# An encoder layer in hi/low fp32 parts: the residual of the down stage spread over more steps, a norm's bias added with the first eviction, the low parts on VectorE, loads kept one fewer ahead, and one norm moved into the middle stage

## The chip, the cores and the metric

The kernel runs on one core of one Trainium2 chip. The metric is the device time of one execution in microseconds (us). Before the change the median of 3 runs is 1983.87 us, from 1979.57 to 1990.23. The engines are named as the profile names them: PE is TensorE (matmul), PEld its weight loads, DVE VectorE, ACT ScalarE, POOL GpSimd, SP SyncE, whose queue issues the DMAs of this kernel.

## The reference

One encoder layer is computed for two independent sequences (s = 0, 1) of 512 tokens, with model width 1024 and inner width 2816, all in fp32:

```python
h = layer_norm(a * x + 0.5 * swiglu(x, ffn1_wg, ffn1_wu, ffn1_wd), ln1_g, ln1_b)
proj = h @ w_in                      # gq, gk, gv, gr, zf, zb, aq, ak, av
o_gla = gla_mixer(gq, gk, gv, gr, zf, zb, ...)      # bidirectional gated linear attention
o_att = gqa_mixer(aq, ak, av, q_norm_g, k_norm_g)   # grouped-query attention with rotary positions
mix = concat([o_gla, o_att]) @ w_out
h = layer_norm(a * h + mix, ln2_g, ln2_b)
h = layer_norm(a * h + 0.5 * swiglu(h, ffn2_wg, ffn2_wu, ffn2_wd), ln3_g, ln3_b)
return h + sigmoid(h @ w_pg + b_pg) * (p @ w_pe)
# swiglu(x, w_g, w_u, w_d) = (silu(x @ w_g) * (x @ w_u)) @ w_d;  a = 2 ** 0.25
```

## The kernel before

**Products in three parts.** Each fp32 operand is kept as a high part `hi` (rounded by a copy to fp32r) and a low part `lo = raw - hi`. A product is three matmuls: hi·hi, hi·lo, lo·hi. `split` (L135) makes the two parts: ACT copies the high part (L137), and VectorE or GpSimd subtracts (L138). Loads of weights go through `raw` buffers (L149, DMAs on SP's queue) and their parts into `w` buffers, of which there are six. `prefetch` (L158) keeps four finished `w` pieces and up to three raw loads ahead.

**The stages.** In order of time: the first SwiGLU (up products to about 462 us, down products to about 666 us), the middle (projections, attention, linear attention, output projection, to about 1215 us), the second SwiGLU (up to about 1629 us, down to about 1860 us), and the final gate (to the end).

**The down stage.** It uses a scheme of seven products for each 2x2 block, as in Strassen's method, in the order `ORDER = (0, 1, 4, 5, 6, 3, 2)`. Eleven row pairs of the down weight are dealt with as three groups of three (`GROUPS`) and a tail of two (`TAIL`). Three groups times seven products are 21 steps, n = 0 to 20, each with 4 x 9 = 36 matmuls (L536). For each step and row pair `w_ops` makes the operand that this product needs: for products 4, 5, 6 and 3 GpSimd first adds or subtracts two quarters of the raw rows in place (L269, one operation for each of the three row pairs), then ACT makes the high part and DVE or POOL the low part. `LOW_DOWN = (0, 1, 6, 2)` names the products whose low parts go to DVE; those of 4, 5 and 3 go to POOL. Two of the tail's operations join the steps of the second and third group. At the end of each quarter of a step `evac` moves one PSUM bank into Y: the first time that a piece of Y is written it is a copy on ACT (L526), afterwards an addition on DVE (L523). The banks are two sets of four, `pm` and `pd`.

**The residual.** The input r of the SwiGLU is loaded from DRAM, one 128x1024 tile for each s and t, and added as Y += 2·ALPHA·r (L617, on DVE). In the second down stage r is a normalized tile without its gain and bias, so `affine` first multiplies by a row g (L642) and adds a row b (L643). In `down` these eight pieces, `res(s, t)`, are due at step 4 (s = 0) or 6 (s = 1) and taken at j = 4 and j = 9 of a step, so two in each of the steps 4 to 7.

**The norm and the projections.** When Y is complete, `ln(s)` finds mean and variance and normalizes in place (L639). `flip` transposes Y on PE, applies gain and bias in the transposed form, and splits it into h1T (L661, L662), the operand of the projections. `h1_rows(s)` applies gain and bias to the untransposed rows (L642, L643) and stores them to DRAM as `sp_h`. The projections run in the order akvz(0), aq(0), gr(0), gr(1), akvz(1), ... Each is `tok_group` (L707), 32 positions of 6 matmuls, with its evacuation at the last four pieces; gr's is a SiLU on ACT (L749) into one of three `ev` buffers, which are stored to DRAM as `sp_G` (L744) by SP's queue.

**What sets the order.** The order on PE is written out by hand. A `Ticker` counts positions of the main work, and side work is woven in at positions given as numbers: `main.weave(h1_rows(0), 4, 28)` spreads four pieces up to position 28. On the other engines and on SP's queue the framework's scheduler sets the order when the program is built. Each engine then works its list in order, and an instruction that waits holds up all behind it.

Of the kernel before, what the change touches and what calls it, by code (L numbers as in the profile page):

```python
# [8 lines left out]
F32 = mybir.dt.float32  # L9
# [11 lines left out]
NT = 4  # L21
# [32 lines left out]
LOW_UP = (1, 5, 2)  # L54
LOW_DOWN = (0, 1, 6, 2)

# [14 lines left out]
class Layer:  # L71
# [88 lines left out]
    def prefetch(self):  # L160
        while len(self.ready) < 4 and (self.raws or self.queue):
            r = self.raws.pop(0) if self.raws else self.raw(self.queue.pop(0))
            n = r.shape[1] // 2
            self.ready += [self.piece(r[:, :n]), self.piece(r[:, n:])]
        while len(self.raws) < 3 and self.queue:
            self.raws.append(self.raw(self.queue.pop(0)))
# [157 lines left out]
    def down_work(self, i, place, spare):  # L324
# [21 lines left out]
        def op_tail(p, k):  # L346
# [3 lines left out]
            return None, f  # L350
        out = [load(p, 0) for p in GROUPS[0]] + [load(p, 1) for p in GROUPS[0]]
        for n, gr in enumerate(GROUPS):
            nxt = GROUPS[n + 1] if n + 1 < len(GROUPS) else None
            if n > 0:
                out += [load(TAIL[n - 1], e) for e in range(2)]
            for k in ORDER:
                for j, p in enumerate(gr):
                    out.append(op(p, k))
                    if k == 3 and nxt:
                        out.append(load(nxt[j], 0))  # L360
                    if k == 2 and nxt:
                        out.append(load(nxt[j], 1))
                if n > 0:
                    out.append(op_tail(TAIL[n - 1], k))
        return out

# [143 lines left out]

    def down(self, hs, hp, residual, ln):

# [5 lines left out]
        def evac(s, t, dd, bank):  # L518
# [5 lines left out]
            else:  # L524
                touched.add((s, t, dd))
                nc.scalar.activation(yv, bank, AF.Copy)  # L526

# [18 lines left out]
        for n in range(21):  # L546
# [8 lines left out]
            for j, _ in enumerate(product(k, H, D, NT, lambda m, t: (m, t))):  # L555
                if n >= 3 and j % 5 == 4 and residual:
                    residual[0][0] <= n and residual.pop(0)[1]()
                yield
# [5 lines left out]
        for s in range(2):  # L564
# [6 lines left out]
            if s == 0:  # L571
                self.prefetch()
                next(first)
        for _ in ln(1):
            pass

# [6 lines left out]
    def ffn(self, i, ysrc, ln, have=(), mid=None, rows=None):  # L583
# [18 lines left out]
        with P("hp", 13) as hp:  # L602
# [6 lines left out]
            g = rows(hp) if rows else None  # L609

            def res(s, t):
                r = hp.tile([128, 2, 512], F32R, tag="h", name="r").bitcast(F32).rearrange("p a n -> p (a n)")
                self.nc.sync.dma_start(r, ysrc(s, t))
                if g:
                    self.affine(r, *g)
                y = self.Y[s, t]
                self.nc.vector.scalar_tensor_tensor(y, r, 2.0 * ALPHA, y, ALU.mult, ALU.add)  # L617
            todo = [(4 if s == 0 else 6, lambda s=s, t=t: res(s, t)) for s in range(2) for t in range(NT)]
            yield from self.down(hs, hp, todo, ln)

# [523 lines left out]
def build(tc, d, outs):  # L1144
    nc = tc.nc
    ctx = ExitStack()
    with ctx:
# [36 lines left out]
        with ExitStack() as mctx:  # L1184
# [27 lines left out]
            main.place(first, (1, 5, 9, 13))  # L1212
            main.weave(h1_rows(0), 4, 28)
            main.weave(L.flip(1, 1, "h1T"), 8, 60)
            main.weave(h1_rows(1), 4, 76)

# [69 lines left out]
        def rows2(hp):  # L1286
            t = [hp.tile([128, 1024], F32, tag="h", name="lnr") for _ in range(2)]
            return [L.row(2, j, t[j]) for j in range(2)]
        for s in range(2):
# [8 lines left out]
        with ExitStack() as fctx:  # L1298
# [11 lines left out]
            def finish():  # L1310
                for s in range(2):
                    for dd in range(2):
# [4 lines left out]
                        for t in range(NT):  # L1317
# [5 lines left out]
                            for c in range(0, 512, n):  # L1323
# [9 lines left out]
                                nc.vector.tensor_tensor(gc, gc, L.Y[s, t][:, oc], ALU.add)  # L1333
                                nc.sync.dma_start(outs[s][t * 128:(t + 1) * 128, oc], gc)
            main = Ticker(finish())
            main.place(first, (2, 7, 12, 17))
# [92 lines left out]
```

## Time and profile before

| | |
|---|---|
| median of 3 runs | 1983.87 us |
| lowest, highest | 1979.57, 1990.23 us |
| profiled execution | 1983.58 us |
| its span in the trace | 1981.8 us |
| mean granted TensorE clock | 0.981 of full speed |
| busy in the span: PE, DVE, POOL, ACT | 1879.1, 1367.1, 950.2, 883.4 us |

The trace covers one execution, the one that took 1983.58 us. Its span is 1.8 us shorter, which is what lies around it. Busy time is a sum over stages that differ; what a stage waits for is read from that stage alone. Rows of the timeline give start, duration, engine, line, operation, tiles and count, and in square brackets the idle time before them and what released them.

### The profile page before, as it was taken

To read this page: it belongs to the slowest core of one execution; us is meant where nothing else is said; L and a number is where in the kernel's file an instruction comes from. 1 tells how busy PE (TensorE), PEld (TensorE's weight loads), DVE (VectorE), ACT (ScalarE), POOL (GpSimd) and SP (SyncE) were. 2 spreads that over 40 slices of the span, in tenths; PEclk is the share of its full clock that TensorE was granted. 3 is DMA by queue.
4 is the path that set the end of the run, shared out by engine and by line. 5 is a ranking of instruction groups with operands and counts; after the bars stand their busy time and mean duration, and the time that the engine had idled before them with its cause. 6 is when DMAs were issued, how large, how long until landed. Compare 5 with 4: busy or idle time off the path is not lost. (4 is left out here: it accounts for less than half of the span.)

```text
span 1981.8 us, 25356 instructions
## 1 busy us (share of the span) xinstructions
PE 1879.1 (95%) x8838; PEld 1534.9 (77%) x8838; DVE 1367.1 (69%) x2068; ACT 883.4 (45%) x1670; POOL 950.2 (48%) x710
## 2 busy tenths in 40 slices
PE   7999999999999797989998888999999999799999
PEld 5788888888788686877876667888888888588787
DVE  7856566574656974778778879566566575855973
ACT  5445444444221444757852337445444444221342
POOL 0665565554761254342234343654665555762253
PEclk9999999999999998999999999999999999899999
DMA  4425444478666233222443331435434478576142
GB/s 177 156 105 177 168 150 152 148 288 337 268 248 211 73 126 111 77 80 91 133 143 101 94 117 66 158 109 185 161 141 170 155 297 338 206 267 255 54 128 85
DMA packets 104959, 322.22 MB, mean 163 GB/s; under 512 B 11008, under 2 KB 38400, under 8 KB 99456
## 3 DMA queue, kind: packets, MB, share of 16 engines
q1 hardware_dynamic: 104832, 320.61, 44.9%
q8 instruction: 70, 1.15, 0.2%
q14 instruction: 57, 0.47, 0.1%
HBM read 218.85 MB, written 101.71 MB: 162 GB/s over the span
## 5 line engine op out<-in xcount | busy, mean ns | idle before, releaser
L138 POOL TENSOR_TENSOR w<-raw,w 128x512 fp32r<-128x512 f32 (+1 forms) x372 | 511.4, 1385 | 773.8 <-ACT w L137 714.7
L137 ACT ACTIVATE w<-raw 128x512 fp32r<-128x512 f32 (+1 forms) x586 | 363.5, 624 | 444.5 <-POOL raw L269 107.8
L425 PE MATMUL pm<-X,w 128*128 128x512 f32 x1848 | 435.0, 393 | 11.0 <-ACT X L137 8.2
L269 POOL TENSOR_TENSOR raw<-raw 128x512 f32<-128x512 f32 x240 | 348.0, 1458 | 155.6 <-DMA raw<-in_wgu 81.7
L425 PEld LDWEIGHTS pm<-X,w 128*128 128x128 f32 x1848 | 347.9, 189 | 89.5 <-ACT X L137 8.8
L425 PE MATMUL pd<-X,w 128*128 128x512 f32 x1320 | 309.2, 392 | 2.9 <-DVE w L138 2.2
L138 DVE TENSOR_TENSOR w<-raw,w 128x512 fp32r<-128x512 f32 x214 | 220.3, 1035 | 126.0 <-ACT w L137 116.4
L425 PEld LDWEIGHTS pd<-X,w 128*128 128x128 f32 x1320 | 248.5, 189 | 58.0 <-DVE w L138 3.0
L536 PE MATMUL pm<-w,XB 128*128 128x512 f32 x864 | 202.5, 394 | 5.5 <-POOL w L138 5.4
L707 PE MATMUL pm<-w,h1T 128*128 128x512 f32 (+1 forms) x768 | 183.9, 382 | 22.6 <-ACT gr L749 11.4
L536 PEld LDWEIGHTS pm<-w,XB 128*128 128x128 f32 x864 | 163.3, 190 | 42.8 <-POOL w L138 9.1
L138 DVE TENSOR_TENSOR hs<-sg,hs 128x512 fp32r<-128x512 f32 (+1 forms) x182 | 143.8, 810 | 49.5 <-ACT hs L137 48.4
L137 ACT ACTIVATE hs<-sg 128x512 fp32r<-128x512 f32 (+1 forms) x182 | 98.4, 561 | 164.8 <-DVE sg L391 64.4
L707 PEld LDWEIGHTS pm<-w,h1T 128*128 128x128 f32 x768 | 135.9, 194 | 45.0 <-ACT gr L749 11.7
L536 PE MATMUL pd<-w,XB 128*128 128x512 f32 x648 | 151.2, 393 | 15.5 <-issue 14.8
L536 PEld LDWEIGHTS pd<-w,XB 128*128 128x128 f32 x648 | 122.8, 190 | 42.0 <-issue 15.2
L523 DVE TENSOR_TENSOR Y<-Y,pm 128x512 f32<-128x512 f32 x104 | 70.6, 684 | 61.5 <-PE pm L536 61.3
L523 DVE TENSOR_TENSOR Y<-Y,pd 128x512 f32<-128x512 f32 x88 | 59.9, 684 | 60.0 <-PE pd L536 57.3
L707 PE MATMUL pm<-w,h3T 128*128 128x512 f32 x384 | 90.8, 393 | 0.9 <-DVE h3T L662 0.9
L371 DVE TENSOR_TENSOR sg<-u,pm 128x512 f32<-128x512 f32 x22 | 15.1, 687 | 109.3 <-PE pm L425 109.3
L707 PEld LDWEIGHTS pm<-w,h3T 128*128 128x128 f32 x384 | 71.2, 188 | 15.8 <-DVE h3T L662 1.4
L652 ACT ACTIVATE pd<-pd,c_lnT 128x512 f32<-128x512 f32 x48 | 36.0, 752 | 100.4 <-PE pd L650 100.4
(237 smaller groups left out, 2554.0 us busy)
## 6 DMA issues: line engine op xcount, KB each, us to landing
hs<-hs SPq DMA_DIRECT2D x126, 512.0 KB, 2.6
XB<-hs SPq DMA_DIRECT2D x42, 1536.0 KB, 6.8
raw<-in_wgu SPq DMA_DIRECT2D x88, 512.0 KB, 3.5
raw<-in_wd SPq DMA_DIRECT2D x36, 512.0 KB, 6.4
hs_t<-hs SPq DMA_DIRECT2D x56, 256.0 KB, 2.5
XB<-hs_t SPq DMA_DIRECT2D x26, 512.0 KB, 5.2
raw<-in_wout SPq DMA_DIRECT2D x16, 512.0 KB, 3.6
raw<-in_wpg SPq DMA_DIRECT2D x16, 512.0 KB, 3.5
```

Source lines behind the costliest of these rows:

```text
L137: first = nc.scalar.activation(hi, raw, AF.Copy)
L138: (eng or nc.vector).tensor_tensor(lo, raw, hi.bitcast(F32), ALU.subtract)
L269: (sums or self.nc.gpsimd).tensor_tensor(o(), x(), y(), ALU.subtract)
L371: add = lambda o, x, y: nc.vector.tensor_tensor(o, x, y, ALU.add)
L425: nc.tensor.matmul(bank, w[:, a, kt * 128:(kt + 1) * 128], X[k][:, kt, b], start=(k in (0, 1, 4) and kt == 0 and m == 0), stop=(kt == 3 an ...
L523: nc.vector.tensor_tensor(yv, yv, bank, ALU.add)
L536: nc.tensor.matmul(b[t], h[:, a, t * 128:(t + 1) * 128], d[:, c], start=(k in (0, 4, 1) and g == 0 and x == 0), stop=(g == len(H) - 1 and ...
L652: nc.scalar.activation(p, p, AF.Identity, scale=self.lnT[:, c:c + 1], bias=self.lnT[:, c + 8:c + 9])
L707: nc.tensor.matmul(banks[t][:, :width], x[:, i, t * 128:(t + 1) * 128], w[a][:, j], start=(q == 0 and a == 0 and m == 0), stop=(q == nq - ...
```

## The change

1. All low parts of the down stage go to DVE (`LOW_DOWN = ORDER`).
2. `prefetch` keeps two raw loads ahead instead of three.
3. The tail's loads and operations stand in one list, and two of them are put behind each of the positions from the eleventh on, instead of one operation with every product.
4. The residual uses two fixed tiles `rt`. A load (`fetch`) and an addition (`res`) are separate entries with half steps as due times, taken at j = 5 and j = 11: the first two loads at half step 3, the later ones at 2n+6, the addition at 2n+9, for n = 0 to 7.
5. In the second down stage the bias row is multiplied by 2·ALPHA once and added by DVE with the first eviction, in place of ACT's copy; r is then only multiplied by g.
6. The norm of s = 1 is kept as `self.later`. After the first down stage it runs at position 32 of the projections, behind akvz(0); `h1_rows(0)`, `flip(1)` and `h1_rows(1)` are spread up to positions 48, 84 and 100, before 28, 60 and 76. After the second down stage it runs behind the loads of the final gate.

```diff
-LOW_DOWN = (0, 1, 6, 2)
+LOW_DOWN = ORDER
@@ prefetch
-        while len(self.raws) < 3 and self.queue:
+        while len(self.raws) < 2 and self.queue:
@@ down_work
+        side = [x for p in TAIL for x in [load(p, 0), load(p, 1)] + [op_tail(p, k) for k in ORDER]]
         for n, gr in enumerate(GROUPS):
             nxt = GROUPS[n + 1] if n + 1 < len(GROUPS) else None
-            if n > 0:
-                out += [load(TAIL[n - 1], e) for e in range(2)]
-            for k in ORDER:
+            for m, k in enumerate(ORDER):
...
-                if n > 0:
-                    out.append(op_tail(TAIL[n - 1], k))
-        return out
+                if 7 * n + m >= 10:
+                    out += side[:2]
+                    del side[:2]
+        return out + side
@@ down, evac
                 touched.add((s, t, dd))
-                nc.scalar.activation(yv, bank, AF.Copy)
+                if rows:
+                    nc.vector.tensor_tensor(yv, bank, rows[1][:, dd * 512:(dd + 1) * 512], ALU.add)
+                else:
+                    nc.scalar.activation(yv, bank, AF.Copy)
@@ down
-                if n >= 3 and j % 5 == 4 and residual:
-                    residual[0][0] <= n and residual.pop(0)[1]()
+                if j in (5, 11) and residual and residual[0][0] <= 2 * n + j // 6:
+                    residual.pop(0)[1]()
...
-        for _ in ln(1):
-            pass
+        self.later = ln(1)
@@ ffn
+            rt = [hp.tile([128, 1024], F32, tag="h", name="r") for _ in range(2)]
+            def fetch(s, t):
+                self.nc.sync.dma_start(rt[t % 2], ysrc(s, t))
             def res(s, t):
-                r = hp.tile([128, 2, 512], F32R, tag="h", name="r").bitcast(F32).rearrange("p a n -> p (a n)")
-                self.nc.sync.dma_start(r, ysrc(s, t))
+                y, r = self.Y[s, t], rt[t % 2]
                 if g:
-                    self.affine(r, *g)
-                y = self.Y[s, t]
+                    self.nc.vector.tensor_tensor(r, r, g[0], ALU.mult)
                 self.nc.vector.scalar_tensor_tensor(y, r, 2.0 * ALPHA, y, ALU.mult, ALU.add)
-            todo = [(4 if s == 0 else 6, lambda s=s, t=t: res(s, t)) for s in range(2) for t in range(NT)]
+            todo = []
+            for n in range(2 * NT):
+                todo += [(2 * n + (6 if n > 1 else 3), lambda a=divmod(n, NT): fetch(*a)), (2 * n + 9, lambda a=divmod(n, NT): res(*a))]
+            todo.sort(key=lambda x: x[0])
@@ build, middle
-            main.weave(h1_rows(0), 4, 28)
-            main.weave(L.flip(1, 1, "h1T"), 8, 60)
-            main.weave(h1_rows(1), 4, 76)
+            main.to(32)
+            for _ in L.later:
+                pass
+            main.weave(h1_rows(0), 4, 48)
+            main.weave(L.flip(1, 1, "h1T"), 8, 84)
+            main.weave(h1_rows(1), 4, 100)
@@ build, rows of the second norm
+            nc.vector.tensor_scalar(g[1], g[1], 2.0 * ALPHA, None, op0=ALU.mult)
@@ build, final gate, behind the loads of pT
+            for _ in L.later:
+                pass
```

The lines of the changed kernel stand 8 further down in this region: L642 and L643 are L650 and L651, L662 is L670, L744 is L752, L799 is L807. Where the scheduler puts the work is shown at three places.

**POOL in the second down stage**, steps 7 to 14 or so. L269 are the in-place sums, L138 the low parts; `raw` and `w` belong to the groups, `dr` and `dt` to the tail. Before:

```order
L269 TENSOR_TENSOR raw<-raw 128x512 x6
L269 TENSOR_TENSOR dr<-dr 128x512 x2
L138 TENSOR_TENSOR w<-raw,w 128x512
L269 TENSOR_TENSOR raw<-raw 128x512
L138 TENSOR_TENSOR w<-raw,w 128x512 x2
L269 TENSOR_TENSOR raw<-raw 128x512 x5
L138 TENSOR_TENSOR dt<-dr,dt 128x512
L269 TENSOR_TENSOR dr<-dr 128x512 x2
L138 TENSOR_TENSOR w<-raw,w 128x512 x3
L138 TENSOR_TENSOR dt<-dr,dt 128x512
```

With the change, the whole of the second down stage on POOL:

```order
L269 TENSOR_TENSOR raw<-raw 128x512 x24
L269 TENSOR_TENSOR dr<-dr 128x512 x4
L269 TENSOR_TENSOR raw<-raw 128x512 x6
L269 TENSOR_TENSOR dr<-dr 128x512 x2
L269 TENSOR_TENSOR raw<-raw 128x512 x6
L269 TENSOR_TENSOR dr<-dr 128x512 x2
```

Only the sums are left there; the low parts stand in DVE's list.

**DVE in the second down stage**, at the residual. Before, around step 7 (Y_138.. and Y_139.. are tiles of s = 1):

```order
L523 TENSOR_TENSOR Y_13793<-Y_13793,pm 128x512
L617 SCALAR_TENSOR_TENSOR Y_13889<-r,Y_13889 128x1024
L642 TENSOR_TENSOR r<-r,lnr 128x1024
L138 TENSOR_TENSOR dt<-dr,dt 128x512
L643 TENSOR_TENSOR r<-r,lnr 128x1024
L642 TENSOR_TENSOR r<-r,lnr 128x1024
L617 SCALAR_TENSOR_TENSOR Y_13900<-r,Y_13900 128x1024
L643 TENSOR_TENSOR r<-r,lnr 128x1024
L523 TENSOR_TENSOR Y_13760<-Y_13760,pd 128x512
L617 SCALAR_TENSOR_TENSOR Y_13911<-r,Y_13911 128x1024
```

With the change, at the densest place:

```order
L138 TENSOR_TENSOR w<-raw,w 128x512
L621 TENSOR_TENSOR r<-r,lnr 128x1024
L523 TENSOR_TENSOR Y_13876<-Y_13876,pd 128x512
L621 TENSOR_TENSOR r<-r,lnr 128x1024
L523 TENSOR_TENSOR Y_13887<-Y_13887,pd 128x512
L622 SCALAR_TENSOR_TENSOR Y_13887<-r,Y_13887 128x1024
L523 TENSOR_TENSOR Y_13898<-Y_13898,pd 128x512
L622 SCALAR_TENSOR_TENSOR Y_13898<-r,Y_13898 128x1024
L523 TENSOR_TENSOR Y_13909<-Y_13909,pd 128x512
L138 TENSOR_TENSOR w<-raw,w 128x512 x3
```

Before, six operations of the residual and one low part stand between two evictions of banks (L523); now no more than one operation of the residual stands between two.

**SP's queue in the projections.** `in_wgr` and `in_wakv` are weights of gr and akvz, `sp_h` the stores of the rows of h1 (83 to 86 of s = 0, 87 to 90 of s = 1), `sp_G` the stores of gr. Before:

```order
L149 DMA raw<-in_wgr 128x1024 x4
L744 DMA sp_h_87<-Y_3645 128x1024
L744 DMA sp_h_88<-Y_3656 128x1024
L149 DMA raw<-in_wgr 128x1024
L744 DMA sp_h_89<-Y_3667 128x1024
L744 DMA sp_h_90<-Y_3678 128x1024
L149 DMA raw<-in_wgr 128x1024 x2
L149 DMA raw<-in_wakv 128x576
L744 DMA sp_G_5097<-gr 128x512
L744 DMA sp_G_5098<-gr 128x512
```

With the change:

```order
L149 DMA raw<-in_wgr 128x1024 x6
L752 DMA sp_h_87<-Y_3648 128x1024
L752 DMA sp_h_88<-Y_3659 128x1024
L752 DMA sp_G_5064<-gr 128x512
L752 DMA sp_G_5065<-gr 128x512
L752 DMA sp_h_89<-Y_3670 128x1024
L752 DMA sp_G_5066<-gr 128x512
L752 DMA sp_G_5067<-gr 128x512
L752 DMA sp_h_90<-Y_3681 128x1024
L149 DMA raw<-in_wakv 128x576 x4
```

The first store of gr stands behind two rows of s = 1 instead of behind four and a load of akvz. DVE, which makes these rows, has them behind the rotary steps of aq(0); before, it had them ahead of these.

More of the change, by code (lines that the diff above doesn't have):

```diff
@@ L509, in stat, with down @@
         self.nc.vector.bn_stats(self.st[s][:, t, dd], self.Y[s, t][:, dd * 512:(dd + 1) * 512])
-    def down(self, hs, hp, residual, ln):
+    def down(self, hs, rows, residual, ln):
         nc = self.nc
@@ L609, in ffn @@
             g = rows(hp) if rows else None
+            rt = [hp.tile([128, 1024], F32, tag="h", name="r") for _ in range(2)]
+            def fetch(s, t):
+                self.nc.sync.dma_start(rt[t % 2], ysrc(s, t))
             def res(s, t):
-                r = hp.tile([128, 2, 512], F32R, tag="h", name="r").bitcast(F32).rearrange("p a n -> p (a n)")
-                self.nc.sync.dma_start(r, ysrc(s, t))
+                y, r = self.Y[s, t], rt[t % 2]
                 if g:
-                    self.affine(r, *g)
-                y = self.Y[s, t]
+                    self.nc.vector.tensor_tensor(r, r, g[0], ALU.mult)
                 self.nc.vector.scalar_tensor_tensor(y, r, 2.0 * ALPHA, y, ALU.mult, ALU.add)
-            todo = [(4 if s == 0 else 6, lambda s=s, t=t: res(s, t)) for s in range(2) for t in range(NT)]
-            yield from self.down(hs, hp, todo, ln)
+            todo = []
+            for n in range(2 * NT):
+                todo += [(2 * n + (6 if n > 1 else 3), lambda a=divmod(n, NT): fetch(*a)), (2 * n + 9, lambda a=divmod(n, NT): res(*a))]
+            todo.sort(key=lambda x: x[0])
+            yield from self.down(hs, g, todo, ln)
     def row(self, i, j, t):
@@ L1287, in rows2 @@
             t = [hp.tile([128, 1024], F32, tag="h", name="lnr") for _ in range(2)]
-            return [L.row(2, j, t[j]) for j in range(2)]
+            g = [L.row(2, j, t[j]) for j in range(2)]
+            nc.vector.tensor_scalar(g[1], g[1], 2.0 * ALPHA, None, op0=ALU.mult)
+            return g
         for s in range(2):
```

## The prediction

> **What bounds the kernel now.** PE is busy nearly throughout, so I looked for the places where it is not. The first view is that of the waits, for PE behind 455 us (waiting engine and line, what it waited for; total, times, longest).
>
> ```profile
> PE pd L536 <- issue: 14.8, 1, 14.8
> PE pm L707 <- ACT gr L749: 11.4, 1, 11.4
> PE pm L707 <- DVE V L821: 8.3, 1, 8.3
> ...
> PE pm L536 <- POOL w L138: 5.4, 3, 4.8
> ```
>
> Two of the four lie in the down stages (L536), two at the start of the projections (L707). A wait leaves out the time that PE loses through a low clock, so I priced the down stages by counts of matmuls, from windows (length, busy time and count for PE, PEld, DVE, ACT and POOL, then the granted clock).
>
> ```profile
> 350.00:400.00 50.00, 50.00 (x221) 41.04 (x220) 28.92 (x32) 22.51 (x40) 27.58 (x20) 1.00 0.42 159
> 520.00:530.00 10.00, 5.78 (x26) 4.46 (x24) 3.79 (x6) 3.16 (x6) 9.84 (x8) 1.00 0.29 121
> 530.00:540.00 10.00, 9.29 (x27) 6.52 (x28) 5.87 (x6) 0.18 (x1) 5.64 (x4) 0.66 0.78 316
> 1700.00:1710.00 10.00, 2.70 (x12) 1.89 (x11) 10.00 (x6) 1.89 (x3) 10.00 (x6) 0.88 0.46 171
> 1710.00:1720.00 10.00, 2.48 (x6) 2.02 (x7) 10.00 (x8) 0.00 (x0) 9.92 (x5) 0.50 0.00 0
> 1720.00:1730.00 10.00, 10.00 (x42) 8.20 (x42) 5.72 (x10) 3.05 (x5) 6.50 (x6) 0.94 0.10 29
> ```
>
> A matmul takes 50/221 = 0.226 us where nothing is in the way, so a step of 36 takes 8.15 us. In 520 to 540 us 53 ran where 88.4 had room: 35.4 x 0.226 = 8.0 us lost. In 1700 to 1730 us 12 + 6 + 42 = 60 of 132.6 ran: 16.4 us lost. These are all that the down stages have to give. In the last three windows DVE and POOL are both full; the timeline of the place (start, duration) shows what on.
>
> ```profile
> 1701.81 0.67 DVE L523 TENSOR_TENSOR Y<-Y,pm 128x512 f32<-128x512 f32 x1
> ...
> 1705.23 10.52 POOL L269 TENSOR_TENSOR raw<-raw 128x512 f32<-128x512 f32 x5
> 1706.27 1.75 DVE L138 TENSOR_TENSOR dt<-dr,dt 128x512 fp32r<-128x512 f32 x1
> ...
> 1712.34 2.28 DVE L617 SCALAR_TENSOR_TENSOR Y<-r,Y 128x1024 f32<-128x1024 f32 x1
> ...
> 1716.75 0.68 DVE L523 TENSOR_TENSOR Y<-Y,pd 128x512 f32<-128x512 f32 x1
> 1717.52 10.19 PE L536 MATMUL pd<-w,XB 128*128 128x512 f32 x36 [14.82 <-issue]
> ```
>
> The view calls the releaser "issue", but the eviction of a pd bank at 1716.75 ends at 1717.43 and PE writes pd at 1717.52: PE waited for a bank. That eviction stood in DVE's list behind six operations of the residual and a low part, from 1701.81 on, each about twice as long as elsewhere:
>
> ```profile
> 1639.86 1.29 POOL L269 TENSOR_TENSOR raw<-raw 128x512 f32<-128x512 f32 x1
> ...
> 1655.60 1.22 DVE L642 TENSOR_TENSOR r<-r,lnr 128x1024 f32<-128x1024 f32 x1
> ...
> 1729.07 0.68 DVE L138 TENSOR_TENSOR w<-raw,w 128x512 fp32r<-128x512 f32 x1
> ```
>
> An operation of the residual takes 2.28 in the burst and 1.22 outside, a low part 1.75 and 0.68, a sum on POOL 10.52/5 = 2.10 and 1.29. The two engines slow each other.
>
> **Down stages.** The change ends this burst: no more than one residual operation stands between two evictions. It also takes all low parts off POOL, which leaves that engine three sums a step and one or two of the tail's. The groups of the second down stage (busy, mean ns) give the price.
>
> ```profile
> L523 DVE TENSOR_TENSOR Y<-Y,pm 128x512 f32<-128x512 f32 x48 | 32.6, 684 | 26.0 <-PE pm L536 25.9
> L138 DVE TENSOR_TENSOR w<-raw,w 128x512 fp32r<-128x512 f32 x33 | 30.0, 917 | 14.8 <-ACT w L137 14.8
> ...
> L617 DVE SCALAR_TENSOR_TENSOR Y<-r,Y 128x1024 f32<-128x1024 f32 x8 | 13.8, 1724 | 0.1
> L643 DVE TENSOR_TENSOR r<-r,lnr 128x1024 f32<-128x1024 f32 x8 | 13.5, 1684 | 0.0
> L642 DVE TENSOR_TENSOR r<-r,lnr 128x1024 f32<-128x1024 f32 x8 | 13.0, 1624 | 0.0
> ```
>
> POOL at its busiest: five sums of 1.29 to 2.10 are 6.5 to 10.5 us against 8.15, and only in a few steps. DVE per step in the second stage: four evictions 4 x 0.684 = 2.7; three low parts at 0.68 to 0.92, 2.0 to 2.8; one or two of the tail's, 0.7 to 1.8; one multiplication and one addition of the residual at 1.22 to 1.72 each, 2.4 to 3.4. Sum 7.8 to 10.7, middle 9.3, which is 1.1 more than PE's 8.15. The additions run through steps 4 to 11 and the tail's operations begin a step or two before the eleventh; with the heaviest steps of the residual I count five such steps: 5.5 us. A step's low parts are made while the one before is computed (six w buffers, three per step), so some of a step is slack; between 0 left (all of it covers) and 8 (5 x the 2.6 of the upper sum, 13, less 5 of slack) I take 3, because the middle sum lies nearer to the slack. The residual loads are part of it: fetched 1.5 steps, 12.2 us, ahead of use, and the next fetch waits for the addition two pieces back to free its tile. The loads took this long to land in 1640 to 1740 us:
>
> ```profile
> r<-sp_z SPq DMA_DIRECT2D x7, 512.0 KB, 9.7
> ```
>
> So 2.5 us are to spare; behind a late one on DVE queue the evictions and low parts of the next step. The second stage then gains 16.4 - 3 = **13.4 us** (8.4 to 16.4). In the first stage r needs no multiplication, so DVE's middle sum is 7.8, below 8.15; the pause there ended on a low part from POOL, 4.8 us, which no longer is POOL's. Left 1 (0 to 4): **7.0 us** (4 to 8).
>
> The bias: 16 first evictions move to DVE at 0.684, 10.9 us, in steps without a residual but the first, where its sum is 2.7 + 2.8 = 5.5; eight L643 of 1.68, 13.5 us, go. One multiplication of the row by 2·ALPHA is at most the 2.28 of a long row, before the first eviction. Price 0, covered by PE's steps; without cover 2.3.
>
> By the Trainium skill, "SBUF — State Buffer", section "Who interferes with whom", a VectorE instruction with two SBUF inputs contends with a GpSimd instruction that reads SBUF, and the second waits for the whole first. The long operations above agree. By that rule the low parts meet the sums on whichever engine they are: four sums, four low parts and two residual operations at 1.29, 0.68 and 1.22 would be 10.3 us in a row, 2.2 over a step, and over four steps 8.6 us would stay in place of 3: 1957.8 for the whole.
>
> **Middle.** Here the pause that ends last governs; the one on V ahead of it only shifts work into it. The timeline at its end:
>
> ```profile
> 745.81 1.29 DVE L799 TENSOR_TENSOR qr<-qr,qk0y 128x512 f32<-128x512 f32 x2
> ...
> 751.91 3.41 DVE L807 TENSOR_TENSOR qr<-qr,sw 128x512 f32<-128x512 f32 x2
> ...
> 753.56 4.41 SPq L744 DMA_DIRECT2D sp_G<-gr  x4
> 757.03 0.60 ACT L749 ACTIVATE gr<-pm 128x512 f32<-128x512 f32 x1 [15.25 <-DMA sp_G<-gr]
> ...
> 757.68 0.80 PE L707 MATMUL pm<-w,h1T 128*128 128x512 f32 x1 [11.43 <-ACT gr L749]
> ```
>
> ACT's fourth eviction of gr waits for an ev buffer, so for the first store, which SP issues only at 753.56, behind a weight load and behind the rows of s = 1. DVE reaches the rotary steps late, because it first does eight row operations for s = 1 and waits for transposes (groups in 714 to 732 us; what the low parts of h1T waited for in 700 to 716):
>
> ```profile
> L642 DVE TENSOR_TENSOR Y<-Y,lnr 128x1024 f32<-128x1024 f32 x4 | 7.0, 1773 | 0.8 <-PE pd L650 0.8
> L643 DVE TENSOR_TENSOR Y<-Y,lnr 128x1024 f32<-128x1024 f32 x4 | 5.3, 1337 | 0.0
>   ACT h1T L661: 6.2, 3
> ```
>
> After the change these eight (7.0 + 5.3 = 12.3 us) stand behind the rotary steps. The 6.2 of waits should go too, since PE is no longer held by V for 8.3 us: the norm's operations for s = 1 come after V's. So L799 starts at 745.81 - 12.3 - 6.2 = 727.3; the rotary steps end 751.91 + 3.41 - 745.81 = 9.5 later, 736.8. Then come four row operations, which the two stores sp_h ahead of the first sp_G need: 4 x 12.3/8 = 6.2, 743.0. The store lands 757.03 - 753.56 = 3.5 later and PE resumes 0.65 behind, at 747.1. Gain 757.68 - 747.1 = 10.6, **11 us**. Lower end: the 6.2 stay, 4.8. Upper end: the pause on gr goes altogether and with it V's, 11.4 + 8.3 = 19.7. I take 11, because the four row operations stand in the list ahead of the store: a wait on gr remains, as PE gets there at 757.68 - 19.7 = 738.0, of some 9 us. The low clock behind pauses I leave in the bounds.
>
> **Loads one later.** Only the loads that `prefetch` makes are meant: projections, output projection, final gate.
>
> ```profile
> raw<-in_wgu SPq DMA_DIRECT2D x88, 512.0 KB, 3.5
> ```
>
> A load of this size lands in 3.5 us; four finished pieces last two pairs of 48 matmuls, 96 x 0.226 = 21.7 us. Price 0; without that cover 3.5 for a late load. The norm of s = 1 at the end moves behind DMA issues that nothing on DVE needs: 0.
>
> **Sum.** 7.0 + 13.4 + 11 = 31.4 us from the profiled 1983.58 gives 1952.2; that execution lies 0.3 us below the median 1983.87, so both serve. With all ends: 1983.6 - 4 - 8.4 - 4.8 = 1966.4, and 1983.6 - 8 - 16.4 - 19.7 = 1939.5.
>
> **Rivals.** First: the gr pause goes as well, if DVE reaches the row operations some 9 us sooner than I think. For it speaks that the norm of s = 1 leaves the stretch before V; against it the fixed list, in which four row operations precede the store. 1952.2 - 8.7 = 1943.5. Second: the middle does not do what it says, because the stores of gr now wait for rows of s = 1 as late as before. For it: two rows are ahead of the first pair of stores, and two more between it and the last; 1952.2 + 11 = 1963.2. Third, on the other side: DVE becomes the pace of the down stages. If low parts take the burst's 1.75 and residual operations 2.28 throughout, a residual step is 2.7 + 5.25 + 2.28 = 10.2 in the first stage and 12.5 in the second; over eight steps each, 17 + 35 = 52 us, so 1983.6 - 8.0 - 16.4 - 11 + 52 = 2000. Against it: 33 low parts averaged 0.92 with POOL carrying its own low parts as well. To lose the whole gain needs 35.4/16 = 2.2 us per step; with residual operations at 1.7 that is a low part of about 1.7 us. Fourth: the down pauses only move, to the steps with residual and tail together; the middle's gain alone remains, 1972.6, or 1968.6 with 4 of the 24.4.
>
> **Chances.** Forecast 0.58, no pause on gr 0.14, no gain in the middle 0.14, pauses moved 0.08, DVE the pace 0.06. The own range, 1939.5 to 1966.4, is widened to 1936 to 1970, which takes in the first, second and half of the fourth. Half a per cent, 10 us, is about what a measurement can tell from no change; faster means below 1974. Faster: 0.58 + 0.14 + 0.14 and most of the fourth, less a little for what I don't see, 0.87; same 0.07; slower 0.06.
>
> **What would show it.** The 14.8 on L536 and the POOL wait are gone and no wait of L536 is above 5. POOL has no low part in the down stages, and its busy time falls by some 66 x 1.29 = 85 us (33 low parts a stage, each of the size of an undisturbed sum). PE's wait on V is below 4, that on gr is still there with 5 to 15. Wrong would be: a wait of L536 on DVE's low parts in steps 8 to 12 that adds up to over 10 us; low parts averaging over 1.2 us on DVE; no wait on gr, or one beyond 20; waits for raw loads in the output projection or the final gate.

## The result, and the profile after

The change makes the kernel faster: 1952.56 us median of 4 runs (1948.34 to 1958.21) against 1987.05 us for the kernel before (1979.57 to 1991.74), a ratio of 0.9843 with a 95% interval of 0.9816 to 0.9871. The forecast was 1952, counted from 1983.6; by these medians the gain is 34.5 us where 31.4 was forecast. The profiled execution after took 1953.48 us with a span of 1951.7 us, 30.1 us less than before.

The span can be cut at the first matmul of each stage. Start times are read from the timelines of PE; the forecast's terms stand beside them. Before the change the stages begin at 442.8, 666.2, 1194.2, 1629.1 and 1859.9 us; the 462 and 1215 us given above for the ends of the first up products and of the middle are about 20 us too late.

| stretch | before, us | after, us | difference | forecast |
|---|---|---|---|---|
| first up products | 442.8 | 440.7 | -2.1 | 0 |
| first down stage | 223.4 | 213.1 | -10.3 | -7.0 |
| projections, to the end of the gr pause | 91.4 | 83.6 | -7.8 | -11 |
| rest of the middle | 436.6 | 439.6 | +3.0 | 0 |
| second up products | 434.9 | 437.2 | +2.3 | 0 |
| second down stage | 230.8 | 214.5 | -16.3 | -13.4 |
| final gate | 121.9 | 123.0 | +1.1 | 0 |
| sum | | | -30.1 | -31.4 |

The two down stages gave more than forecast, the projections less. The three stretches without a change moved by 2 to 3 us either way. In the kernels below they lie between 440.4 and 445.6 us (first up products), 436.8 and 440.8 (rest of the middle, e1 to e7) and 434.9 and 439.5 (second up products), so these differences are within what one execution differs from the next.

The view of the waits for PE behind 455 us, after the change (waiting engine and line, what it waited for; total, times, longest):

```profile
PE pm L715 <- ACT gr L757: 9.9, 1, 9.9
...
PE pm L715 <- DVE V L829: 4.1, 1, 4.1
...
PE pm L539 <- DVE Y L523: 2.9, 4, 1.0
...
PE pd L658 <- DVE Y L647: 1.7, 2, 1.3
```

The 14.8 and 5.4 us of the down stages (now L539) are gone. The wait on V is half of what it was, and the wait on gr has hardly changed. The windows at the places of the old pauses (length, busy time and count for PE, PEld, DVE, ACT, POOL, then the granted clock):

```profile
530.00:540.00 10.00, 10.00 (x45) 8.27 (x45) 8.03 (x12) 4.83 (x9) 2.59 (x2) 1.00 0.69 256
1680.00:1690.00 10.00, 10.00 (x46) 8.28 (x45) 10.00 (x10) 1.71 (x3) 9.84 (x5) 1.00 0.62 215
1690.00:1700.00 10.00, 10.00 (x46) 8.29 (x45) 9.93 (x11) 3.58 (x6) 1.71 (x2) 1.00 0.59 224
1700.00:1710.00 10.00, 9.67 (x43) 7.71 (x42) 10.00 (x14) 2.53 (x4) 2.92 (x2) 1.00 1.02 418
1710.00:1720.00 10.00, 9.51 (x43) 7.54 (x42) 8.53 (x13) 3.23 (x6) 2.60 (x2) 1.00 0.45 166
```

PE runs 43 to 46 matmuls in 10 us at full clock, where 12 and 6 ran before. DVE is as full as before in the second stage, yet PE hardly waits: no more than one operation of the residual now stands between two evictions, and from 1690 us on DVE finishes 11 to 14 operations in 10 us where it finished 6 to 8, with POOL busy for 1.7 to 2.9 us in place of 10. From 1680 to 1690 us both engines are full, and PE runs on at 46 matmuls all the same. The groups of the second down stage (from 1611 us on) show what DVE and POOL paid (busy, mean ns):

```profile
L138 DVE TENSOR_TENSOR w<-raw,w 128x512 fp32r<-128x512 f32 x60 | 53.3, 906 | 5.8 <-ACT w L137 5.6
...
L622 DVE SCALAR_TENSOR_TENSOR Y<-r,Y 128x1024 f32<-128x1024 f32 x8 | 11.7, 1461 | 0.2
L621 DVE TENSOR_TENSOR r<-r,lnr 128x1024 f32<-128x1024 f32 x8 | 11.3, 1415 | 0.0
...
L269 POOL TENSOR_TENSOR raw<-raw 128x512 f32<-128x512 f32 x32 | 52.2, 1647 | 60.1 <-DVE w L138 58.4 <-DMA raw<-in_wd 0.7
```

The operations are still longer than undisturbed ones (0.68, 1.22 and 1.29 us). POOL, without its low parts, now stands idle for 58.4 us until a low part on DVE has read the raw rows that the next sum overwrites.

What a down stage loses can be read step by step, from the first of a step's 36 matmuls to the first of the next. An undisturbed step takes 8.16 us. In the first stage before, step 2 took 1.0 us more, step 10 8.5 and step 17 0.9, 10.4 in all; with the change no step is longer. In the second stage before, step 8 took 15.0 more, step 9 1.9 and step 17 0.9, 17.7 in all; with the change 1.4 are left, in steps 11 and 12. The waits behind the losses of the first stage before:

```profile
461.52 6.91 PE L536 MATMUL pd<-w,XB 128*128 128x512 f32 x29 [0.65 <-POOL w L138]
...
530.61 14.74 PE L536 MATMUL pm<-w,XB 128*128 128x512 f32 x49 [4.84 <-POOL w L138]
...
593.31 1.89 PE L536 MATMUL pm<-w,XB 128*128 128x512 f32 x7 [0.30 <-POOL w L138]
```

Those left in the second stage after:

```profile
1708.60 6.42 PE L539 MATMUL pm<-w,XB 128*128 128x512 f32 x27 [0.33 <-DVE Y L523]
1715.51 6.41 PE L539 MATMUL pm<-w,XB 128*128 128x512 f32 x27 [0.49 <-DVE Y L523]
```

### The profile page after: what moved, and what is told of

It reads as the page before. It is cut to its first block, busy times and chain, and to the rows that moved or that the text cites. A ratio compares the mean times of both kernels' runs of the same rounds, so it can differ in the third digit from the quotient of the medians.

```text
span 1951.7 us, 25305 instructions
## 1 busy us (share of the span) xinstructions
PE 1877.6 (96%) x8838; PEld 1535.1 (79%) x8838; DVE 1413.1 (72%) x2143; ACT 873.8 (45%) x1654; POOL 860.5 (44%) x644
## 5 line engine op out<-in xcount | busy, mean ns | idle before, releaser
L138 POOL TENSOR_TENSOR w<-raw,w 128x512 fp32r<-128x512 f32 (+1 forms) x318 | 431.8, 1367 | 750.3 <-ACT w L137 685.6
L269 POOL TENSOR_TENSOR raw<-raw 128x512 f32<-128x512 f32 x240 | 355.9, 1491 | 227.4 <-DVE w L138 155.6
L425 PEld LDWEIGHTS pm<-X,w 128*128 128x128 f32 x1848 | 347.2, 188 | 89.7 <-ACT X L137 8.6
L138 DVE TENSOR_TENSOR w<-raw,w 128x512 fp32r<-128x512 f32 x268 | 263.2, 990 | 115.5 <-ACT w L137 111.6
L539 PE MATMUL pm<-w,XB 128*128 128x512 f32 x864 | 198.4, 389 | 0.8 <-DVE Y L523 0.8
L539 PEld LDWEIGHTS pm<-w,XB 128*128 128x128 f32 x864 | 162.0, 188 | 35.2 <-DVE Y L523 1.7
L138 DVE TENSOR_TENSOR hs<-sg,hs 128x512 fp32r<-128x512 f32 (+1 forms) x182 | 145.4, 818 | 49.6 <-ACT hs L137 48.4
L715 PEld LDWEIGHTS pm<-w,h1T 128*128 128x128 f32 x768 | 136.3, 195 | 36.5 <-ACT gr L757 10.1
L539 PE MATMUL pd<-w,XB 128*128 128x512 f32 x648 | 148.8, 389 | 0.0
L539 PEld LDWEIGHTS pd<-w,XB 128*128 128x128 f32 x648 | 121.6, 188 | 25.2
L523 DVE TENSOR_TENSOR Y<-Y,pm 128x512 f32<-128x512 f32 x104 | 70.4, 682 | 36.1 <-PE pm L539 36.0
L523 DVE TENSOR_TENSOR Y<-Y,pd 128x512 f32<-128x512 f32 x88 | 58.7, 678 | 19.3 <-PE pd L539 19.3
```

What stands on the lines that cost most here:

```text
L138: (eng or nc.vector).tensor_tensor(lo, raw, hi.bitcast(F32), ALU.subtract)
L269: (sums or self.nc.gpsimd).tensor_tensor(o(), x(), y(), ALU.subtract)
L425: nc.tensor.matmul(bank, w[:, a, kt * 128:(kt + 1) * 128], X[k][:, kt, b], start=(k in (0, 1, 4) and kt == 0 and m == 0), stop=(kt == 3 an ...
L523: nc.vector.tensor_tensor(yv, yv, bank, ALU.add)
L539: nc.tensor.matmul(b[t], h[:, a, t * 128:(t + 1) * 128], d[:, c], start=(k in (0, 4, 1) and g == 0 and x == 0), stop=(g == len(H) - 1 and ...
L715: nc.tensor.matmul(banks[t][:, :width], x[:, i, t * 128:(t + 1) * 128], w[a][:, j], start=(q == 0 and a == 0 and m == 0), stop=(q == nq - ...
```

## The experiments

**The low parts back on POOL, all else as changed (e1).**

```diff
-LOW_DOWN = ORDER
+LOW_DOWN = (0, 1, 6, 2)
```

> The change with one part undone: the low parts of products 4, 5 and 3 are POOL's again in both down stages. Theory (two causes: in the second stage the residual's burst on DVE, in the first a low part late on POOL): the second down stage stays near the changed kernel's 214.5 us, up to 4 longer; the first grows from 213.1 by 4 to 8 with a wait of L539 on POOL's low parts; the whole is 5 to 12 us slower than the change, about 1961. Rival (POOL's load, which makes DVE's operations long, is the cause of both pauses): the second stage grows by 10 to 16 as well, the whole is about 1975.

Measured: 1963.87 us (ratio to before 0.9906, 0.9875 to 0.9937), 11 us more than the change. First stage 216.7 us (+3.6), second 222.3 (+7.8). Waits of PE in the second stage:

```profile
PE pm L539 <- POOL w L138: 3.3, 4, 1.5
PE pm L539 <- DVE Y L523: 1.0, 1, 1.0
PE pm L539 <- ACT w L137: 1.0, 1, 1.0
```

The second stage lost more than the theory of two separate causes allowed (4) and less than the rival wanted (10 to 16). The waits on parts of w name 4.3 of the 7.8 us; behind them the granted clock is 0.56 from 1700 to 1705 us and 0.76 in the next 5 us.

**The burst back, the low parts left on DVE (e2).** The residual is dealt as before the change, with gain and bias on r and first evictions on ACT.

```diff
-                if j in (5, 11) and residual and residual[0][0] <= 2 * n + j // 6:
+                if n >= 3 and j % 5 == 4 and residual:
```

> The change with the residual as before: two pieces a step in steps 4 to 7, gain and bias both on r, first evictions on ACT; the low parts stay on DVE. Theory (the burst is the cause in the second stage): a pause of 10 to 25 us comes back there, longer than the 14.8 of before if anything, since DVE now has three more low parts a step; the first stage grows by 2 to 8; the whole about 1975. Rival (POOL's load was the cause): without low parts on POOL the residual's operations are nearer to 1.22 than to 2.28 us, the pause is below 5, and the whole is within 5 us of the change.

Measured: 1959.34 us (0.9876, 0.9841 to 0.9911). First stage 213.1, no loss; second 221.0 (+6.5), with a pause of 5.1 us in place of 14.8. The timeline at that pause:

```profile
1692.55 3.62 POOL L269 TENSOR_TENSOR raw<-raw 128x512 f32<-128x512 f32 x2 [18.45 <-DVE w L138]
1694.38 10.91 PE L539 MATMUL pd<-w,XB 128*128 128x512 f32 x36 [5.14 <-issue]
```

The groups of the burst's operations (gain and bias on r) in that stage:

```profile
L645 DVE TENSOR_TENSOR r<-r,lnr 128x1024 f32<-128x1024 f32 x8 | 9.7, 1216 | 0.0
L644 DVE TENSOR_TENSOR r<-r,lnr 128x1024 f32<-128x1024 f32 x8 | 9.6, 1214 | 0.0
```

This went the rival's way, though the pause and the whole, 7 us above the change, lie just beyond the 5 that it allowed. With the low parts on DVE, POOL's next sum must wait until DVE has read the raw rows; it idled for 18.45 us while the burst ran, and the burst's operations took 1.21 us each where before they took 1.62 to 1.72 on average and 2.28 at the pause. So the 14.8 us of before were neither the burst's nor POOL's alone: the burst was long because POOL worked through it, and with POOL waiting 5.1 us of the pause remain.

**The middle as before (e3).**

```diff
-            main.to(32)
-            for _ in L.later:
-                pass
-            main.weave(h1_rows(0), 4, 48)
+            main.weave(h1_rows(0), 4, 28)
```

and so on for the other two lines, with the norm of s = 1 at the end of the first down stage.

> The change with the norm of s = 1 at the end of the first down stage again and the rows and transposes at positions 28, 60 and 76. Theory: the wait on V returns to about 8 us and the gr pause to about 11; from the first matmul of the projections to the end of the gr pause 91 us in place of 83.6; the whole 5 to 9 us slower than the change. Rival (the gr pause only fills up with what is saved ahead of it, and the middle gained nothing that lasts): that stretch differs by less than 2 us and the whole by less than 3.

Measured: 1957.76 us (0.9871, 0.9835 to 0.9906), 5 us more than the change. The stretch to the end of the gr pause is 90.9 us against 83.6, as the theory said. The pause on gr is 11.4 us; the wait on V came back only to 4.5, with 2.9 on a low part of h1T beside it. The size of that wait says little here: it is 4.5 in e5 too, whose middle is the one of before, while aq(0) begins 25.9 us after the stage's start in e3, 24.8 in e5, 26.9 before and 18.9 with the change.

**Three raw loads ahead again (e4).** `len(self.raws) < 2` becomes `< 3`.

> The change with three raw loads ahead again in place of two. Theory (prefetch is covered by four finished pieces, 21.7 us): no stage differs by more than 2 us, the whole is within 4 us of the change either way. Rival (the loads one later let SP's queue pass the stores of rows and of gr sooner, or cost waits in the output projection and the gate): the start of the projections or the final stage differs by 3 to 8 us.

Measured: 1951.72 us (0.9841, 0.9806 to 0.9876). No stage differs by more than 2.3 us from the change's, and that is the second up stage, whose weights are not loaded by `prefetch`. In the whole the loads one later are worth nothing that these runs can tell, but the rival shows in small: the pause on gr is longer than the 9.8 to 9.9 us of the change and of e1, e2, e6 and e7. PE's wait, and SP's queue ahead of it:

```profile
PE pm L715 <- ACT gr L757: 11.4, 1, 11.4
```

```profile
731.91 1.46 SPq L752 DMA_DIRECT2D sp_h<-Y  x2
733.48 0.40 SPq L149 DMA_DIRECT2D raw<-in_wakv  x1
733.92 1.45 SPq L752 DMA_DIRECT2D sp_G<-gr  x2
```

A load of akvz stands between the rows and the first stores of gr, and PE goes on 84.1 us after the stage's start, against 82.4 to 82.6 in those four kernels (the change, at 83.6, had lost 1.1 us more in aq(0)): about 1.5 us. The cover was smaller than the expectation says: a group of the projections is 96 matmuls, so a position of the `Ticker` has 3 of them and not 6, a pair of pieces serves 24, and four pieces last 48 x 0.226 = 10.8 us and not 21.7.

**The low parts alone, on the kernel before (e5).** The one line `LOW_DOWN = ORDER`.

> The kernel before with one part of the change alone: all low parts of the down stages on DVE. The first runs gave: with the lows back on POOL the second stage is 222.3 us, with the burst back 221.0, with neither 214.5, and before, with both, 230.8. Theory now (two engines slow each other, so each of the two parts gives about half): the second stage comes to 220 to 223 with a pause of some 5, the first to 213 to 216, the projections stay as before; the whole 14 to 19 us below before, about 1966. Rival (the old tail and loads share in it, so that the part alone gives less): the second stage stays above 226, or the first above 218.

Measured: 1967.89 us (0.9903, 0.9874 to 0.9931). First stage 214.4, as expected: here the low parts alone bring 9.0 of the 10.3 us. Second stage 224.7, between theory and rival, with a pause of 8.6 where 5 was expected. With e1 this gives the second stage in full: 230.8 with both the burst and POOL's low parts, 224.7 with the burst alone, 222.3 with POOL's low parts alone (and the rest of the change), 214.5 with neither. Taking one away brings 6.1 or 8.5, taking both 16.3; the two add up to 14.6, so 1.7 us hang on taking both. In the first stage they overlap: the low parts alone bring 9.0, the rest of the change without them (e1) 6.7, both 10.3.

**The tail dealt as before (e6)**, one operation with every product.

> The change with the tail's loads and operations dealt as before, one with each product of the second and third group. Theory: it moves one operation a step and carries nothing; both down stages within 2 us of 213.1 and 214.5, the whole within 4 us of the change. Rival (the first stage's gain of 10.3, which neither low parts nor burst explain alone, hangs on the tail): the first stage 217 or more.

Measured: 1952.19 us (0.9835, 0.9810 to 0.9859); first stage 213.1, second 215.8. The whole cannot be told from the change. The second stage can: in the seven kernels with the change's down stages (e3, e4, e8 to e12) it takes 214.4 to 214.7 us, and here steps 9 and 10 lose 1.3 us each where steps 11 and 12 lose 1.4 together. So the tail's new order is worth about 1.3 us.

**The bias on r again (e7)**, first evictions on ACT, residual spread.

```diff
-                    self.nc.vector.tensor_tensor(r, r, g[0], ALU.mult)
+                    self.affine(r, *g)
```

> The change with the bias added to r again (the residual stays spread, first evictions on ACT). DVE then has one more operation of 1.2 to 1.7 us in each of eight steps of the second stage and 16 x 0.68 us less in the first steps. Theory (DVE is full from step 6 to 12 but not the pace): the second stage 214.5 plus 0 to 4. Rival (DVE is at its limit there): plus 5 to 12, with waits on low parts or banks.

Measured: 1956.35 us (0.9846, 0.9823 to 0.9869); second stage 214.8 (+0.3). Eight more long operations on DVE there, with 16 evictions fewer in the steps before, cost nothing that these runs can tell, although DVE is full.

**The stores of gr from ACT's queue (e8).**

```diff
-            self.put("G", s, t, g)
+            self.nc.scalar.dma_start(self.spill["G", s][t], g)
```

> The change, with the stores of gr issued from ACT's queue, behind the activation that makes gr, and no longer from SP's behind the rows of s = 1. Theory (the pause on gr comes from the order of SP's queue): the fourth eviction waits only for the first store, 3.5 us, while the evictions are 1.36 us apart; the pause of 9.9 falls below 2, the stretch from the first projection to that place shrinks from 83.6 to about 74, and the whole to about 1943. Rival (PE would stop there anyway, for weights or for the transposes of s = 1 that DVE makes late): a wait of another name takes 5 to 10 us at the same place, and the whole stays within 4 us of the change.

Measured: 1953.56 us (0.9842, 0.9814 to 0.9869). The pause on gr is gone and another stands in its place. The new wait of PE in the middle:

```profile
PE pd L879 <- DVE K L886: 7.5, 1, 7.5
```

The rival held. PE's next transposes need the bank that K's low part frees, and this stands behind the eight row operations of s = 1 in DVE's list (timeline):

```profile
725.88 3.95 DVE L650 TENSOR_TENSOR Y<-Y,lnr 128x1024 f32<-128x1024 f32 x2
729.75 2.35 DVE L651 TENSOR_TENSOR Y<-Y,lnr 128x1024 f32<-128x1024 f32 x2
732.02 2.34 DVE L650 TENSOR_TENSOR Y<-Y,lnr 128x1024 f32<-128x1024 f32 x2
734.29 3.42 DVE L651 TENSOR_TENSOR Y<-Y,lnr 128x1024 f32<-128x1024 f32 x2
737.63 1.37 DVE L886 TENSOR_TENSOR K<-pd,K 64x512 fp32r<-64x512 f32 x2
```

SP's queue was how the delay reached PE, not where it arose: it arose in DVE's list.

**The normalization of s = 1 on ACT (e9)**, added to e8.

```diff
-                    L.ln_z(s, t, m, r)
+                        nc.scalar.activation(y, y, AF.Identity, scale=r[:, t:t + 1], bias=nb[:, t:t + 1])
```

> As e8_gr_store, and the normalization of s = 1 (four L647 of 128x1024, 6.3 us on DVE) on ACT, as scale and bias of an activation. In e8 the pause on gr went and one of 7.5 us on K took its place, since K's low part stands behind eight row operations on DVE. Theory (DVE's list is what PE waits for from 654 to 740 us; relieving DVE of 6 us ahead of V moves all behind it): the wait on V, 4.1 us, falls below 1; the pause on K stays at 5 to 8, because PE comes there as much earlier as DVE does; the whole 3 to 5 us below e8 and the change, about 1948. Rival (DVE has slack there and the chain through the rotary steps sets it): the wait on V goes, the pause on K grows by the same 4, and the whole does not move.

Measured: 1951.90 us (0.9839, 0.9811 to 0.9866). Neither was right in full: the wait on V went from 4.1 to 3.5 only, since the scheduler moved the rows of s = 0 up to where the four operations had been, and the pause on K stayed at 7.4.

**Half of the row operations on POOL (e10)**, added to e9: the multiplications of the rows of s = 1.

> As e9, and the multiplication of the four rows of s = 1 by the gain on POOL instead of DVE. Theory (DVE's eight row operations at about 1.8 us are the pause on K): DVE has four left, POOL's four of about 2.6 us (twice an undisturbed sum of half the size) run from the end of the rotary steps, so the rows are ready some 3 to 5 us earlier; the pause on K falls to 2 to 5, the whole to about 1945. Rival (POOL's low parts for gr(1) come behind these four and are late): a wait of L715 on POOL's low parts of 4 to 10 us, and the whole is no better than e9 or worse.

Measured: 1952.23 us (0.9843, 0.9813 to 0.9873). The rival held: no wait on K, 1.3 us on gr, but

```profile
PE pm L715 <- POOL w L138: 5.7, 3, 3.5
```

**K before the rows of s = 1 (e11)**, added to e8. K's transposes come at position 98, the rows behind them, Q's tiles are taken one by one.

```diff
-            main.weave(h1_rows(1), 4, 100)
-            main.to(PLAN["s0"])
-            main.weave(M.qk_stacks(0, q0, o0[0], (None, 0, 1, 2, 3)), 5, PLAN["s1"])
+            main.to(98)
+            stacks = M.qk_stacks(0, q0, o0[0], (None, 0, 1, 2, 3))
+            next(stacks)
+            main.weave(h1_rows(1), 4, 104)
+            main.weave(stacks, 4, 114)
```

In `h1_rows(1)` the affine is issued after K's last low part (`tc.issue_after`), and K's tiles are allocated ahead of Q's.

> As e8, and K's parts made before the rows of s = 1: K's transposes at position 98, its two tiles from the buffers that the rows of s = 0 left, the rows of s = 1 behind K's low parts in DVE's list, Q's four tiles taken one by one behind them. Theory (the pause on K is only the order on DVE: eight row operations ahead of four small ones): the pause of 7.5 us goes, a smaller wait of up to 4 appears where Q waits for the rows' stores, the middle gets 4 to 7 us shorter than in e8, the whole 4 to 7 below the change, about 1947. Rival (DVE and POOL are full from 654 to 740 us, so that whichever operation stands behind the rows is late): the wait goes to another name at about the same place and size, and the whole stays within 3 us of the change, as e8, e9 and e10 did.

Measured: 1938.48 us (1932.86 to 1942.07), a ratio to before of 0.9776 (0.9753 to 0.9799), an interval clear of the change's 0.9816 to 0.9871. K's low parts now stand ahead of the rows in DVE's list:

```profile
728.59 1.38 DVE L891 TENSOR_TENSOR K<-pd,K 64x512 fp32r<-64x512 f32 x2
731.24 1.40 DVE L891 TENSOR_TENSOR K<-pd,K 64x512 fp32r<-64x512 f32 x2 [1.27 <-ACT K L889]
732.67 4.16 DVE L650 TENSOR_TENSOR Y<-Y,lnr 128x1024 f32<-128x1024 f32 x2
```

The timeline of PE from K's transposes to Q's last:

```profile
726.72 0.60 PE L884 MATMUL pd<-c_ident,kr 128*128 128x128 f32 x4
727.08 4.36 PE L715 MATMUL pm<-w,h1T 128*128 128x512 f32 x18
...
737.45 0.60 PE L884 MATMUL pd<-c_ident,qr 128*128 128x128 f32 x4
737.80 12.62 PE L715 MATMUL pm<-w,h1T 128*128 128x512 f32 x57
```

No pause is left there; the only wait of PE from 650 to 760 us is the one on V, 4.1 us. The middle took 509.8 us, 519.9 in e8 and 523.2 with the change: 10.1 less than e8 where the theory said 4 to 7, and the smaller wait at Q did not come. Nearly all of it lies at this place, since akvz(1) begins 92.0 us after the stage's start where it was 101.5 in e8. K's transposes also come four positions sooner and the tiles of K and Q are allocated in another order, which was not tried apart from the order on DVE. This version beats both kernels: about 45 us below before and 14 below the change by the medians.

**The norm of s = 1 and the rows of s = 0 behind V (e12)**, added to e11.

> As e11, and the norm of s = 1 and the rows of s = 0 behind V's low parts in DVE's list. e9 took the four L647 off DVE and the wait on V stayed at 3.5, because the rows of s = 0 took their place ahead of V. Theory: with all of these behind V the wait of 4.1 falls below 1; what DVE did there it now does while PE is in aq(0), so the later waits grow by at most 2; the whole 2 to 4 below e11. Rival (DVE's sum of work up to K sets the time): the wait on V goes and the waits behind grow by as much; the whole equals e11 within 2.

Measured: 1944.44 us (0.9824, 0.9801 to 0.9847), worse than e11. The wait on V is gone, and this one has come:

```profile
PE pd L658 <- DVE Y L647: 9.4, 4, 8.7
```

The scheduler now interleaves the rows of s = 0 with the small operations of the norm, and the transposes of s = 1 wait for it. A wait of 4.1 us was exchanged for one of 8.7, and akvz(1) begins 99.1 us after the stage's start in place of 92.0.

## Why the prediction was right, and where its terms were off

**The sum** was right to 0.6 us by the medians, with terms that erred both ways. Sign and causes were forecast, but the closeness is chance: in the profiled executions the down stages gave 10.3 + 16.3 = 26.6 us where 20.4 stood, and the rest of the span gave 30.1 - 26.6 = 3.5 where 11 stood.

**First down stage**: forecast 7.0, measured 10.3. The term was mis-sized twice. The 8.0 us of 520 to 540 us were called all that this stage had to give, while it lost 10.4: 8.5 in step 10, and 1.9 in steps 2 and 17, at two other places where PE waited for a low part from POOL. And of the 1 us left in place nothing can be seen: the only wait of L539 there is 1.0 us on an eviction, which was there before.

**Second down stage**: forecast 13.4, measured 16.3. Here too the windows had missed some of the loss: it was 17.7 us and not 16.4, of which 0.9 lay in step 17. (In the last of the three windows DVE and POOL were not both full, as the prediction says, but busy for 5.72 and 6.50 us of 10.) And the 3 us left in place were too many: 1.4 are left, in steps 11 and 12, and 17.7 - 1.4 = 16.3. DVE was full from 1680 to 1710 us as worked out (10.00, 9.93 and 10.00 us busy in the windows above), but PE waited for it only in these two steps, 0.3 and 0.5 us: up to there the slack, which I had put at 5 us, was larger than the surplus. How large was not measured.

**The cause in the second stage** was told as the burst on DVE, each operation about twice as long because the two engines slow each other. e1, e2 and e5 bear out both halves: either part alone brings 6 to 9 us, both 16.3, and the burst's operations take 1.21 us when POOL stands still. My first theory for the experiments, the burst as the one cause there, fell.

By the Trainium skill, "SBUF — State Buffer", section "Who interferes with whom", the low parts and sums meet on either engine, and 8.6 us would have stayed. The lengthening is still there in the trace (sums at 1.65 us, low parts at 0.91), but only 1.4 us stayed in the stage's time. What that sum left out is an order between the two: a sum in place waits for the low part that reads its rows, 58.4 us in all, and while it waits it does not disturb (e2). From 1680 to 1690 us they do meet, with operations of the residual at 1.7 to 2.3 us, and there the slack covers them. How much of the 8.6 each of the two accounts for was not tried.

**Middle**: forecast 11, measured 7.8. The chain of the forecast holds link by link, counted from the stage's start. The rotary multiplication (L799 before, now L807) came at 715.78 - 653.80 = 62.0 us where 727.3 - 666.2 = 61.1 was forecast; the rows of s = 1 took longer and began behind one more low part of h1T:

```profile
715.78 1.29 DVE L807 TENSOR_TENSOR qr<-qr,qk0y 128x512 f32<-128x512 f32 x2
...
720.20 10.79 POOL L138 TENSOR_TENSOR w<-raw,w 128x512 fp32r<-128x512 f32 x6
...
725.36 0.68 DVE L670 TENSOR_TENSOR h1T<-pd,h1T 128x512 fp32r<-128x512 f32 x1
725.96 3.91 DVE L650 TENSOR_TENSOR Y<-Y,lnr 128x1024 f32<-128x1024 f32 x2
729.79 3.42 DVE L651 TENSOR_TENSOR Y<-Y,lnr 128x1024 f32<-128x1024 f32 x2
...
733.61 1.41 SPq L752 DMA_DIRECT2D sp_G<-gr  x2
736.77 0.60 ACT L757 ACTIVATE gr<-pm 128x512 f32<-128x512 f32 x1 [13.00 <-DMA sp_G<-gr]
737.42 2.93 PE L715 MATMUL pm<-w,h1T 128*128 128x512 f32 x6 [9.86 <-ACT gr L757]
```

Four row operations took 7.3 us in place of 6.2, with POOL's low parts running beside them at 1.8 us each. The remaining wait on gr, forecast at some 9 us, is 9.9. Of the signs named ahead, POOL's busy time fell by 950.2 - 860.5 = 89.7 us (85 forecast) and no wait of L539 is above 5; the wait on V, 4.1, just missed its bound of 4. The step that was mis-sized is the end of the chain, 80.9 us after the stage's start where 83.6 was measured. That the order on SP's queue holds PE there was shown by e8 as far as the path goes; the source is DVE's list (e8 to e11).

**Loads one later, tail, bias**: priced at nothing, and in the whole e4, e6 and e7 cannot tell them from nothing. At their places two of them are worth something: the loads one later take about 1.5 us off the pause on gr, by way of SP's queue, and the tail's order 1.3 us off the second down stage.

**The norm at the end** was priced at 0 because nothing on DVE needs the DMAs that it moves behind. It costs about 1 us: the final stage takes 122.6 to 123.3 us in all kernels that have it and 121.9 in before and in e5, and PE's waits on the normalized Y (L647), 1.7 us, are new there. What I left out is PE: its transposes of s = 1 need the norm.

## What to carry to other kernels

When two engines are both full at a pause, ask whether each is full because of the other, and try the parts one at a time as well as together: here either part alone brought a third to a half of what the second stage gained, and in the first stage they overlapped. A pause moves along in-order lists to whatever stands next behind the same work, as the one on gr went to K and then to POOL's low parts; it went away only when the work itself, eight row operations, was put behind the few small operations that PE waited for (e11). A loss is counted over the whole stage, step by step, and not in the windows around the longest waits alone. And where a forecast comes out right, compare its terms too: here three of them missed by about 3 us each, in both directions.

## What was not expected of the hardware

A VectorE operation on 128x1024 took 1.21 us or 2.3 us by what GpSimd did at the time, and the difference was decided by an order between the engines: in the burst of e2, with POOL waiting, every operation took 1.21.

The times of one kernel's executions go with the granted clock. The four of the changed kernel were 1948.34, 1951.63, 1953.48 and 1958.21 us, at mean clocks of 0.990, 0.986, 0.985 and 0.983. Why the clock differs between executions of the same program was not tried. It bears on how these studies are read: these four lie 10 us apart, so a gain of 5 us at one pause can vanish in the whole, while the stretch from stage to stage shows it (the first down stage took 213.1 us in the change and in eight of the kernels above).
